# Two ratios and one weight of the filler order in the mixer stage of a two-layer hybrid encoder

## The chip, the core and the metric

The kernel runs on one core of a Trainium2 chip. TensorE (PE in the profile) does the matmuls, VectorE (DVE) and ScalarE (ACT) the elementwise work, GpSimd (POOL) a few masks and powers, SyncE (SP) issues most DMAs. The metric is the device time of one execution in microseconds; the time before is the median of three runs.

## The reference

The input is 256 tokens of width 1024 (fp32), and there are two layers. Each layer is

```
x = x + 0.5 * rms_norm(swiglu(rms_norm(x)))          # feed-forward, width 2816
z = rms_norm(x) @ w_in                                # one wide projection
y = concat(conv(z), retention(z), rwkv7(z), mlstm(z)) @ w_out
x = x + rms_norm(y)
x = x + 0.5 * rms_norm(swiglu(rms_norm(x)))          # second feed-forward
```

The four mixers have 256 channels each (4 heads of 64). All of them read columns of the same z:

```
conv:      zb * (conv1d_width3(zc * zh) + bias)                    # three projections of 256 columns
retention: rotary q, k; decay masks forward and backward; rms norm of the heads, silu gate
rwkv7:     a state S per head, forward and backward over the 256 tokens:
           S = S * w_t - (S kk_t)(kk_t a_t)^T + v_t k_t^T ;  out_t = S r_t
           then group norm, bonus and gate
mlstm:     chunks of 128; weights exp(d_log - running max) from input and forget gates,
           (q k^T * weights) v over a normalizer, forward and backward
```

## The kernel before

Everything stays on chip; the weights stream through. A 512 KB piece of a weight matrix comes by DMA on SP's queue into one of four raw buffers, ACT casts it to a rounded "hi" part and DVE forms the rest as "lo" (line 259), and every large product is done as hi x hi + hi x lo + lo x hi (three matmuls). PE's order of work is the main thing that the kernel decides. A planner places the instructions: program order is their priority, and an instruction that the planner's own estimate does not have ready lets a later one pass.

A layer is feed-forward, mixers, feed-forward. In the mixer stage the RWKV recurrence is the long chain of small dependent steps. It is solved in blocks of 64 tokens (four blocks, n = 0 to 3, two directions d): masked products of keys and queries (pgr), a triangular inverse built from 16x16 pieces (L937 pe, L949, L955, L976, L985, each a flood of 32x32 tiles), pakv (L997), and then the chain proper: pwc, pu, psn and oT (L1013 to L1053), where each step reads the state that the step before left. After it come RWKV's norm and gate (L1061 on).

The other three mixers are written as Python generators, and so is RWKV. Each `yield` hands back a weight, meant as the TensorE time in us of what was just emitted. In the first half (up to "quads", after L937) RWKV runs beside `fill1`, in the second beside `fill2`:

```
fill2 = seq_(mix(seq_((1.0 for i in range(1)), ro, mlstm()), conv(), R2), project())
```

Two ratios set the order in `fill2`. The loop over `rwkv()` adds up RWKV's weights (tm) and the weights of what was emitted beside it (tf), and once `RATIO2 * tm` is `GRAIN` (0.8) ahead of tf it emits from `fill2` until it has caught up. Inside, `mix` runs retention's end (ro) and mLSTM as its first and conv as its second part: conv is emitted until its own sum has reached `R2` times that of the first. What is left of `fill2` when RWKV has been emitted is drained behind it.

Names that the change and the prediction touch:

- conv (L1272): six projections of 128 columns, pz (L388): 8 k's of three matmuls each, a yield of 0.64 every two k's; after three of them an elementwise block (up, yc) on DVE and ACT.
- mlstm (L1161): waits (yield 0.3) until RWKV's side has formed MR, the gates' running maxima; then four broadcasts of two matmuls each, pmb (L1174 and 1175), which ACT turns into the weights wf and wfh; scores pss (L1097), products pom (L1214), and `finish`, whose transposes are ptf (L786).
- project (L1337): the first rows of w_out, ym (L1334), which read the mixers' outputs yT in the order retention, conv, mLSTM, RWKV.

PSUM has two buffers "d" (pz, later y of the first 128 tokens), two "a" (pmb, pss, pom, later y of the second), three "y" for RWKV and one "o".

Of the kernel before, what the change touches and what calls it, by code (L numbers as in the profile page):

```python
# [105 lines left out]
def tile_encoder(ctx: ExitStack, tc: tile.TileContext, x_in, wffn, win, wout, gains, params, idn, cst, rel, out, dbg=None):  # L106
# [13 lines left out]
    def tt(out, a, b, op, eng=V):  # L120
        eng.tensor_tensor(out=out, in0=a, in1=b, op=op)  # L121

    def mul(out, a, b, eng=V):
        tt(out, a, b, ALU.mult, eng)

    def add(out, a, b, eng=V):
        tt(out, a, b, ALU.add, eng)
# [10 lines left out]
    def stt(out, a, s, b, op0, op1):  # L138
        V.scalar_tensor_tensor(out=out, in0=a, scalar=s, in1=b, op0=op0, op1=op1)

    def act(out, a, f, **kw):
        return A.activation(out, a, f, **kw)  # L142
# [10 lines left out]
    def m4(shape, dt=F32, name="m4"):  # L153
        return bigp.tile(shape, dt, tag="m4", bufs=13, name=name)
# [10 lines left out]
    def a1(name, shape=(P, S), dt=F32):  # L165
        return sp.tile(list(shape), dt, tag="a1", bufs=3, name=name)

    def dump(name, ap):
        if name in dbg:
            nc.sync.dma_start(out=dbg[name], in_=ap)  # L170
# [19 lines left out]
    def c_(n):  # L190
        o, w = _COFF[n]
        return C[:, o:o + w]
# [200 lines left out]

    TA, TB, TC, SG = 4, 2, 7, 2
    NPRO, NEPI, SPLITC, WARM, W_FIN, ZW = 3, 7, 4, 6, 6.0, 2
    RATIO, RATIO2, W_PREP, W_INV, GRAIN, R1, R2, WQ, QG, KD = 0.8, 0.6, 8, 12, 0.8, 1.4, 1.2, 0.12, 8, 2

    def ffn(hold, l, j, XT, before1, before2, ahead, after, first, last, mix_next):

# [177 lines left out]
    def mixers(hold, l, XT, before2, ahead, after):  # L577
# [193 lines left out]
        def finish(o_, gate, m, scale=None, tag="a"):  # L771

            sq_ = m4([P, 2, S], name="sq_")
            act(sq_, o_, AF.Square, scale=0.125)
            ms = sp.tile([P, 8], F32, tag="ms8", bufs=2, name="ms8")
            red(ms, sq_.rearrange("p a (h v) -> p (a h) v", v=HD))
            ts(ms, ms, RMS_EPS, ALU.add)
            r = rstd(ms, 8, "r8")
            mul(gate, gate, o_)
            g4 = gate.rearrange("p a (h v) -> p (a h) v", v=HD)  # L780
            mul(g4, g4, r.rearrange("p (h o) -> p h o", o=1).broadcast_to([P, 8, HD]))
            yield W_FIN
            pt = ps.tile([P, 2, S], F32, tag=tag, bufs={"a": PA, "o": 1}[tag], name="ptf")
            for c in range(2):
                for tk in range(2):
                    T.transpose(pt[:, c, tk * P:(tk + 1) * P], gate[:, tk, c * P:(c + 1) * P], ident)  # L786
            new_yt(m)
            if scale is None:
                split_out(yT[m], pt)
            else:  # L790
                for c in range(2):
                    act(yT[m][:, 0, c, :], pt[:, c, :], AF.Copy, scale=scale[:, c:c + 1])
                    stt(yT[m][:, 1, c, :], pt[:, c, :], scale[:, c:c + 1], f(yT[m][:, 0, c, :]), ALU.mult, ALU.subtract)
# [298 lines left out]
        def scores(t, sk, name):  # L1092

            pq = [ps.tile([P, 2, S], F32, tag="a", bufs=PA, name=f"{name}{hp}") for hp in range(2)]
            for p in range(2):
                for hp in range(2):
                    T.matmul(pq[hp][:, p, :], lhsT=t[half[hp], 2 + p, sk * P:(sk + 1) * P], rhs=t[half[hp], p, :],  # L1097
                             start=p == 0, stop=True, skip_group_check=True)
            yield 0.86
            return pq  # L1100
# [60 lines left out]
        def mlstm():  # L1161
            while "MR" not in hold:
                yield 0.3
            MR = hold["MR"]

            toff = [[0, P], [0, 0]]
            tn = [[S, P], [P, S]]
            wfh = m4([P, 2, H, P], name="wfh")
            wf = [[m4([P, H, S], name="wf0"), wfh[:, 0]], [wfh[:, 1], m4([P, H, S], name="wf1")]]
            for d in range(2):  # L1170
                for hp in range(2):
                    pm_ = ps.tile([P, 2, S], F32, tag="a", bufs=PA, name="pmb")
                    for i in range(2):
                        j = 4 * d + 2 * hp + i  # L1174
                        T.matmul(pm_[:, i, :], lhsT=pair[64:128, j:j + 1].broadcast_to([64, P]), rhs=MR[64:128, d, :],
                                 start=i == 0, stop=True, skip_group_check=True)
                    yield 0.22
                    if d == 0 and hp == 0:
                        pc = ps.tile([P, 2, 16], F32, tag="o", bufs=1, name="pc")
                        for tk in range(2):  # L1180
                            T.matmul(pc[:, tk, :], lhsT=gT[:, tk * P:(tk + 1) * P], rhs=c_("sel"), start=tk == 0, stop=True,
                                     skip_group_check=True)
                        V.tensor_copy(out=cc, in_=pc[:, :, 0:8])
                        act(em, pc[:, :, 8:16], AF.Exp, scale=-1.0)
                    for i in range(2):
                        h = 2 * hp + i
                        j = 4 * d + h
                        for sk in range(2):
                            t0 = toff[d][sk]
                            act(wf[d][sk][:, h, :], pm_[:, i, t0:t0 + tn[d][sk]], AF.Exp, scale=-1.0,  # L1190
                                             bias=cc[:, sk, j:j + 1])
                for sk in range(2):
                    o0 = sk * P - toff[d][sk]
                    v_ = wf[d][sk][:, :, o0:o0 + P]
                    G.affine_select(out=v_, in_=v_, pattern=[[0, H], [1 if d == 0 else -1, P]], compare_op=ALU.is_ge,
                                    fill=0.0, base=0, channel_multiplier=-1 if d == 0 else 1)
            for sk in range(2):
                pss = yield from scores(mq, sk, "pss")
                for hp in range(2):
                    ps_ = pss[hp]  # L1200
                    for d in range(2):
                        t0 = toff[d][sk]
                        wv = wf[d][sk].rearrange("p (a b) t -> p a b t", b=2)[:, :, hp, :]
                        stt(wv, ps_[:, :, t0:t0 + tn[d][sk]], 0.125, wv, ALU.mult, ALU.mult)
            hsum = m4([P, 2, H, HD], name="hsum")
            for tk in range(2):
                for d in range(2):
                    po = ps.tile([P, H, HD + 1], F32, tag="a", bufs=PA, name="pom")
                    sks = [sk for sk in range(2) if (sk <= tk if d == 0 else sk >= tk)]
                    for h in range(H):  # L1210
                        for sk in sks:
                            o0 = tk * P - toff[d][sk]
                            for c in range(2):
                                T.matmul(po[half[c], h, :], lhsT=wf[d][sk][:, h, o0 + 64 * c:o0 + 64 * c + 64], rhs=v1[:, sk, h, :],  # L1214
                                         start=h == 0 and sk == sks[0], stop=sk == sks[-1], skip_group_check=True)
                        yield 0.17 * len(sks)
                    dn = sp.tile([P, H], F32, tag="dn", bufs=4, name="dn")
                    act(dn, po[:, :, HD], AF.Abs)
                    tt(dn, dn, em[:, tk, 4 * d:4 * d + 4], ALU.max)
                    V.reciprocal(out=dn, in_=dn)  # L1220
                    db = dn.rearrange("p (h o) -> p h o", o=1).broadcast_to([P, H, HD])
                    if d == 0:
                        mul(hsum[:, tk], po[:, :, 0:HD], db)
                    else:
                        ob = a1("ob", (P, H, HD))
                        mul(ob, po[:, :, 0:HD], db)
                        add(hsum[:, tk], hsum[:, tk], ob)

            yield from finish(hsum.rearrange("p a h v -> p a (h v)"), og, 3, PR("mn"), "o")
            if l == 0:  # L1230
                dump("y3", yT[3].bitcast(F32))
# [105 lines left out]
        def project():  # L1337
# [3 lines left out]
            for i, tk in ((0, 0), (1, 0), (2, 0), (3, 0), (0, 1), (1, 1), (4, 0), (5, 0)):  # L1341
# [5 lines left out]
                yield 0.64  # L1347

        fill2 = seq_(mix(seq_((1.0 for i in range(1)), ro, mlstm()), conv(), R2), project())
        tm = tf = 0.0  # L1350
        rest, ratio = fill1, RATIO
# [179 lines left out]
```

## Time and profile before

| what | us |
|---|---|
| median of three runs | 1164.4 |
| the runs | 1164.4, 1154.44, 1165.07 |
| profiled execution, as a whole | 1157.71 |
| its span, first to last instruction | 1156.0 |
| PE busy / DVE busy / ACT busy in the span | 1116.3 / 787.4 / 653.5 |
| mean granted TensorE clock | 0.988 |

The profile is of one execution. In a row of groups stand line, engine, operation, output<-input, tile sizes (rows*columns of the array, then the operand), the count, and behind the bar the busy time in us, the mean duration in ns, and the idle time of the engine before it with what ended it. In a table of stretches stand the stretch (from the span's start, in us), its length, then busy time and count per engine, the granted TensorE clock, the busy share of the DMA engines and GB/s. In the order of time stand start, duration, and the instruction with its count. A row of waits is: who, for whom, us in total, times, longest. Matmuls overlap: the time that one holds the array is read from start to start, and a busy PE is not PE at its peak.

### The profile page before, as it was taken

To read this page: it belongs to the slowest core of one execution; us is meant where nothing else is said; L and a number is where in the kernel's file an instruction comes from. 1 tells how busy PE (TensorE), PEld (TensorE's weight loads), DVE (VectorE), ACT (ScalarE), POOL (GpSimd) and SP (SyncE) were. 2 spreads that over 40 slices of the span, in tenths; PEclk is the share of its full clock that TensorE was granted. 3 is DMA by queue.
4 is the path that set the end of the run, shared out by engine and by line. 5 is a ranking of instruction groups with operands and counts; after the bars stand their busy time and mean duration, and the time that the engine had idled before them with its cause. 6 is when DMAs were issued, how large, how long until landed. Compare 5 with 4: busy or idle time off the path is not lost.

```text
span 1156.0 us, 20352 instructions
## 1 busy us (share of the span) xinstructions
PE 1116.3 (97%) x8083; PEld 954.3 (83%) x8083; DVE 787.4 (68%) x1371; ACT 653.5 (57%) x1193; POOL 51.4 (4%) x87
## 2 busy tenths in 40 slices
PE   8999999999899999999899999999989999999997
PEld 6888887897878788888798888879868778888886
DVE  6666566798867856566666656667895578566663
ACT  7575555777435755454555555568764157555562
POOL 0000000012000000000000000000301000000000
PEclk9999999999999999999999999999998799999999
DMA  7856554432323666655546655625242136665641
GB/s 259 278 188 202 181 189 157 145 125 90 114 72 108 202 222 193 203 174 199 179 149 207 215 186 186 209 73 185 74 159 63 56 127 205 204 196 185 197 163 37
DMA packets 53535, 189.46 MB, mean 164 GB/s; under 512 B 6200, under 2 KB 6848, under 8 KB 53440
## 3 DMA queue, kind: packets, MB, share of 16 engines
q1 hardware_dynamic: 51120, 181.28, 47.8%
q10 hardware_dynamic: 2320, 6.89, 1.8%
q8 instruction: 63, 1.03, 0.3%
q14 instruction: 32, 0.26, 0.1%
HBM read 187.10 MB, written 1.05 MB: 163 GB/s over the span
## 4 chain that ended last, share of the span: by engine, by line
PE 60%; DVE 12%; DMA 12%; ACT 8%; issue 6%; POOL 1%; SPq 0%; POOLq 0%; ACTq 0%; DVEq 0%
PE pg L472 16%; PE y L495 14%; DMA f_raw<-in_wffn_dram 11%; PE pz L388 9%; PE pg L474 8%; DVE f_lo L259 4%; ACT f_hi L142 4%; PE pgh L444 2%; DVE i_lo L259 1%; PE pss L1097 1%; PE pvg L594 1%; PE ym L1334 1%; ACT i_hi L142 1%; ACT jk L142 1%; DVE gu L121 1%
## 5 line engine op out<-in xcount | busy, mean ns | idle before, releaser
L259 DVE TENSOR_TENSOR f_lo<-f_raw,f_hi 128x1024 fp32r<-128x1024 f32 (+1 forms) x280 | 323.0, 1162 | 195.6 <-ACT f_hi L142 194.9
L472 PE MATMUL pg<-XT,f_hi 128*128 128x512 f32 x1232 | 387.4, 396 | 1.4 <-DVE gu L121 1.3
L142 ACT ACTIVATE f_hi<-f_raw 128x1024 fp32r<-128x1024 f32 (+1 forms) x280 | 279.0, 1007 | 137.8 <-DMA f_raw<-in_wffn_dram 116.6
L474 PEld LDWEIGHTS pg<-XT,f_lo 128*128 128x128 f32 x1232 | 231.3, 188 | 54.0
L474 PE MATMUL pg<-XT,f_lo 128*128 128x256 f32 x1232 | 242.2, 278 | 0.0
L495 PE MATMUL y<-f_hi,hT 128*128 128x512 f32 x704 | 232.6, 392 | 3.8 <-ACT hT L142 2.7
L472 PEld LDWEIGHTS pg<-XT,f_hi 128*128 128x128 f32 x1232 | 192.6, 189 | 7.4 <-DVE gu L121 2.2
L495 PEld LDWEIGHTS y<-f_hi,hT 128*128 128x128 f32 x704 | 131.6, 188 | 31.0 <-ACT hT L142 4.0
L388 PE MATMUL pz<-XT,i_hi 128*128 128x256 f32 x704 | 139.8, 295 | 2.2 <-DVE rvg L121 1.4
L495 PE MATMUL y<-f_lo,hT 128*128 128x512 f32 x352 | 137.3, 391 | 0.0
L388 PEld LDWEIGHTS pz<-XT,i_hi 128*128 128x128 f32 x704 | 111.4, 193 | 10.3 <-issue 4.1
L142 ACT ACTIVATE hT<-gu 128x256 fp32r<-128x256 f32 x77 | 32.1, 417 | 130.8 <-DVE gu L121 130.8
L388 PE MATMUL pz<-XT,i_lo 128*128 128x256 f32 x352 | 101.3, 288 | 0.0
L259 DVE TENSOR_TENSOR i_lo<-i_raw,i_hi 128x1024 fp32r<-128x1024 f32 (+1 forms) x68 | 73.6, 1095 | 14.5 <-ACT i_hi L142 13.5
L142 ACT ACTIVATE i_hi<-i_raw 128x1024 fp32r<-128x1024 f32 (+1 forms) x68 | 63.5, 953 | 34.4 <-PE pz L388 22.8
L121 DVE TENSOR_TENSOR gu<-pg,gu 128x256 f32<-128x256 f32 x154 | 64.4, 418 | 16.1 <-ACT gu L142 16.1
L495 PEld LDWEIGHTS y<-f_lo,hT 128*128 128x128 f32 x352 | 66.1, 188 | 11.1 <-DVE f_lo L259 0.4
L444 PE MATMUL pgh<-f_hi,XT 128*128 128x256 f32 x352 | 69.0, 290 | 2.1 <-ACT XT L142 1.1
L388 PEld LDWEIGHTS pz<-XT,i_lo 128*128 128x128 f32 x352 | 68.0, 193 | 0.8 <-issue 0.5
L142 ACT ACTIVATE gu<-pg 128x256 f32<-128x256 f32 x154 | 56.8, 369 | 18.7 <-PE pg L474 18.7
L444 PEld LDWEIGHTS pgh<-f_hi,XT 128*128 128x128 f32 x352 | 56.6, 191 | 5.3 <-ACT XT L142 1.8
L488 DVE TENSOR_TENSOR hT<-gu,hT 128x256 fp32r<-128x256 f32 x77 | 32.8, 425 | 35.1 <-ACT hT L142 34.5
(290 smaller groups left out, 1275.7 us busy)
## 6 DMA issues: line engine op xcount, KB each, us to landing
f_raw<-in_wffn_dram SPq DMA_DIRECT2D x262, 512.0 KB, 4.4
i_raw<-in_win_dram SPq DMA_DIRECT2D x60, 512.0 KB, 4.0
o_raw<-in_wout_dram SPq DMA_DIRECT2D x16, 512.0 KB, 3.7
gain<-in_gains_dram ACTq DMA_DIRECT2D x11, 512.0 KB, 4.9
x<-in_x_dram SPq DMA_DIRECT2D x4, 256.0 KB, 4.3
f_raw<-in_wffn_dram SPq DMA_DIRECT2D x4, 256.0 KB, 5.1
rl<-in_rel_dram ACTq DMA_DIRECT2D x2, 384.0 KB, 3.2
C<-in_cst_dram SPq DMA_DIRECT2D x1, 573.0 KB, 6.9
```

The lines of the kernel that those rows point to most:

```text
L121: eng.tensor_tensor(out=out, in0=a, in1=b, op=op)
L142: return A.activation(out, a, f, **kw)
L259: V.tensor_tensor(out=lo[:, cs], in0=r[:, cs], in1=f(hi[:, cs]), op=ALU.subtract)))
L388: T.matmul(dst, lhsT=w[a][:, k * P:(k + 1) * P], rhs=xt(XT, k, b), start=n == 0, stop=n == 23)
L444: T.matmul(pg, lhsT=xt(XT, k, a)[:, tk * P:(tk + 1) * P], rhs=w[b][:, c:c + 256], start=n == 0, stop=n == 23)
L472: T.matmul(pg, lhsT=w[0][:, c:c + P], rhs=xt2(XT, k + i), start=k + i == 0, stop=False, skip_group_check=True)
L474: T.matmul(pg[:, 0, :], lhsT=w[1][:, c:c + P], rhs=xt(XT, k + i, 0), start=False, stop=k + i == 7, skip_group_check=True)
L488: V.tensor_tensor(out=hT[:, 1, :], in0=h, in1=f(hT[:, 0, :]), op=ALU.subtract))
L495: ins = T.matmul(y[tk][h], lhsT=hts[fb][:, a, tk * P:(tk + 1) * P], rhs=ws[fb][2][b][:, h * 512:(h + 1) * 512], start=fb == 0 and i == 0, ...
L594: T.matmul(pv[tk], lhsT=xt(XT, k, a)[:, tk * P:(tk + 1) * P], rhs=w[b][:, (k % 2) * 512:(k % 2 + 1) * 512], start=k == 0 and i == 0, stop= ...
L1097: T.matmul(pq[hp][:, p, :], lhsT=t[half[hp], 2 + p, sk * P:(sk + 1) * P], rhs=t[half[hp], p, :], start=p == 0, stop=True, skip_group_check ...
L1334: T.matmul(y[tk][h], lhsT=yT[(1, 0, 3, 2)[i // 2]][:, a, i % 2, tk * P:(tk + 1) * P], rhs=wo[i][b][:, h * 512:(h + 1) * 512], start=i == 0 ...
```

## The change

Three numbers of the second half of the mixer stage change, in both layers:

- RATIO2 0.6 to 0.75: per unit of RWKV's weight, more of `fill2` is emitted beside it.
- R2 1.2 to 1.45: per unit of the weight of retention's end and mLSTM, more of conv is emitted.
- mLSTM's four broadcasts pmb yield 0.5 instead of 0.22 each, so more of conv goes behind each of them, and they use up more of what may be emitted beside RWKV.

No instruction is added or taken away; only the emission order, and with it the planner's order, changes.

```diff
@@ -393,7 +393,7 @@
     NPRO, NEPI, SPLITC, WARM, W_FIN, ZW = 3, 7, 4, 6, 6.0, 2
-    RATIO, RATIO2, W_PREP, W_INV, GRAIN, R1, R2, WQ, QG, KD = 0.8, 0.6, 8, 12, 0.8, 1.4, 1.2, 0.12, 8, 2
+    RATIO, RATIO2, W_PREP, W_INV, GRAIN, R1, R2, WQ, QG, KD = 0.8, 0.75, 8, 12, 0.8, 1.4, 1.45, 0.12, 8, 2
@@ -1174,7 +1174,7 @@
                         T.matmul(pm_[:, i, :], lhsT=pair[64:128, j:j + 1].broadcast_to([64, P]), rhs=MR[64:128, d, :],
                                  start=i == 0, stop=True, skip_group_check=True)
-                    yield 0.22
+                    yield 0.5
```

## The prediction

> **What bounds the kernel now.** I read the page first (busy shares, granted clock), then the busy time by stretch around the second half of each mixer stage, the PE groups inside one thin stretch, what PE waited for, and PE's order of work.
>
> ```profile
> span 1156.0 us, 20352 instructions
> PE 1116.3 (97%) x8083; PEld 954.3 (83%) x8083; DVE 787.4 (68%) x1371; ACT 653.5 (57%) x1193; POOL 51.4 (4%) x87
> PEclk9999999999999999999999999999998799999999
> ```
>
> TensorE is the bound: 97% busy over 1156.0 us; the execution as a whole took 1157.71 us, so 1.7 us lie around the span. The clock row has one dent, in the slices that hold the second half of layer 1's mixers. The diff touches only that half (layer 0: 298 to 382 us; layer 1: 864 to 949).
>
> What PE waits for between 296 and 385 us, layer 0's half with a margin:
>
> ```profile
> PE pt L314 <- DVE xg L301: 1.8, 1, 1.8
> PE ptf L786 <- DVE og L121: 1.1, 1, 1.1
> PE pe L949 <- issue: 0.7, 1, 0.7
> PE pe L955 <- issue: 0.5, 1, 0.5
> PE pe L949 <- DVE En L943: 0.4, 1, 0.4
> PE pe L937 <- ACT Dn L921: 0.3, 1, 0.3
> ```
>
> So 4.8 us per layer is all that better filling could win, and most of it is outside the change's reach: pt belongs to the next norm, L937 and L949's wait for En come before a larger share of conv work is handed out, and "issue" waits for no other engine. Only ptf's 1.1 us hangs on the order in question. In the RWKV chain itself there is nothing to fill, as busy time by stretch shows (columns: length, then busy time of each engine with its count, granted clock, DMA):
>
> ```profile
> core 0: us, PE busy (x) PEld busy (x) DVE busy (x) ACT busy (x) POOL busy (x), PEclk, DMA share, GB/s
> 314.89:322.04 7.15, 7.15 (x145) 5.98 (x144) 3.29 (x6) 4.60 (x16) 1.23 (x2) 1.00 0.26 79
> 322.04:350.00 27.96, 27.96 (x404) 22.03 (x402) 18.06 (x51) 7.65 (x22) 1.36 (x4) 1.00 0.24 74
> 320.05:335.67 15.62, 15.62 (x197) 11.57 (x195) 9.58 (x24) 5.91 (x17) 2.34 (x4) 1.00 0.09 33
> 885.13:912.43 27.30, 27.30 (x197) 19.67 (x195) 10.21 (x25) 5.98 (x17) 2.34 (x4) 0.50 0.05 18
> ```
>
> The last two rows are the same 197 matmuls in layer 0 and in layer 1. With the clock at 1.00 they take 15.62 us, at 0.50 they take 27.30. One such stretch costs 27.30 - 15.62 = 11.7 us (0.75 us per us of covered work), more than twice all the waits of a layer. The clock falls where layer 0 stands at 320.05, which is 5.2 us into the first of these rows, 314.89 to 322.04. There PE does this (busy time, mean ns, idle time before):
>
> ```profile
> L997 PE MATMUL pakv<-UV,GP 64*64 64x64 f32 x64 | 3.4, 226 | 0.0
> L1175 PE MATMUL pmb<-MR,pair 64*128 64x256 f32 x8 | 1.7, 314 | 0.0
> L985 PE MATMUL pe<-D64T,F__3413 32*32 32x32 f32 x64 | 1.4, 192 | 0.0
> L388 PE MATMUL pz<-XT,i_lo 128*128 128x256 f32 x2 | 0.8, 384 | 0.0
> L388 PE MATMUL pz<-XT,i_hi 128*128 128x256 f32 x3 | 0.7, 279 | 0.0
> L1181 PE MATMUL pc<-C,gA 128*128 128x16 f32 x4 | 0.6, 268 | 0.0
> ```
>
> All tiles there are a quarter, a half or a sixteenth of the 128x128 array, but for five pz (conv projections) and the small pc. Layer 0 has the same order and kept its clock. So the fall has a part of chance, and an array thinly used for some microseconds is its likely condition; idle time is not, for there is none.
>
> **How the profiled time stands to the runs.** Runs of 1154.44, 1164.40 and 1165.07 us form two groups 10.3 us apart, close to one 11.7 us stretch. The profile (1157.71, one stretch) lies 0.3% above the lower and 0.6% below the upper group. I read: one stretch at 1154 to 1158, two (one per layer) at 1164 to 1170, none at 1157.7 - 11.7 = 1146.0, or 1143 from the run. That makes 1, 1, 2 and 2 stretches in four executions, 6 of 8 chances.
>
> **The change, part by part.** I walked the weights of the generators by hand. RWKV's steps after "quads" weigh 4 x 3.84 + 4 x 0.8 + 2 x 0.32 + 12.48 = 31.7. A ratio of 0.6 lets 19.0 of other work run beside them, 0.75 lets 23.8. Conv has 6 projections of 8 k's, 3 matmuls each (144). With the new R2 and the heavier broadcasts too, 42 of its 48 k's are handed out before the chain ends, where it was 32; before L976 it is 22, where it was 16. L388's matmuls alone bear the old count out:
>
> ```profile
> 298.00:359.19 61.19, 24.75 (x154) 19.87 (x154) 1.00 0.25 77
> 350.00:359.19 9.19, 4.96 (x37) 4.48 (x36) 1.00 0.03 12
> ```
>
> Of the 154, ten still belong to mLSTM's projections; 154 - 10 - 37 = 107, or 36 k's, lie before 350, where the chain ends. So the planner pulls about four k's ahead of the weights when a small step isn't ready, and my order is right only to about that much.
>
> *What moves at no cost.* No matmul and no DMA is added or removed. Conv's six weight pieces are issued earlier on SP's queue, where only w_out's pieces stand behind them; the gain pieces go through ACT's queue. The cover is that ACT and DVE are far from full in the chain (7.65 and 18.06 of 27.96 us); without it PE would wait for one cast or take the next pom. Conv's first elementwise block moves ahead of the chain, the second stays behind it.
>
> *Cuts.* Evener means more and shorter runs of pz between steps of other tile shapes. PE in order of time (start, duration):
>
> ```profile
> 299.19 0.39 PE L388 MATMUL pz<-XT,i_lo 128*128 128x256 f32 x1
> ...
> 332.30 0.38 PE L388 MATMUL pz<-XT,i_lo 128*128 128x256 f32 x1
> 332.61 0.34 PE L1038 MATMUL psn<-UV,bkT 128*64 128x64 f32 x4
> ...
> 355.89 0.39 PE L1214 MATMUL pom<-v,wf 128*64 128x65 f32 x6
> 356.21 0.51 PE L388 MATMUL pz<-XT,i_hi 128*128 128x256 f32 x2
> ...
> 359.07 0.28 PE L388 MATMUL pz<-XT,i_lo 128*128 128x256 f32 x1
> 359.19 0.40 PE L1334 MATMUL ym<-o_hi,yT 128*128 128x512 f32 x1
> ...
> 363.73 0.66 PE L786 MATMUL ptf<-ident,og 128*128 128x128 f32 x4 [1.15 <-DVE og L121]
> ...
> 373.29 0.61 PE L1334 MATMUL ym<-o_hi,yT 128*128 128x512 f32 x2
> 373.75 0.39 PE L1334 MATMUL ym<-o_lo,yT 128*128 128x512 f32 x1
> 373.97 0.61 PE L1334 MATMUL ym<-o_hi,yT 128*128 128x512 f32 x2
> ```
>
> In the long run from 356.21 to 359.19 a pz starts every 0.12 us (24 in 2.98); the lone one at 332.30 holds the array for 0.31. A run of pz therefore costs about 0.19 us beyond its matmuls. By hand there are 13 such runs before and 17 after; the trace has 25 (the first at 299.19, the last at 356.21), so by the same ratio it would be 33. That gives between nothing, if the planner merges them again, and 8 x 0.19 = 1.5 us per layer. I take 4 x 0.19 = 0.75, the hand count, or 1.5 for both layers (0 to 3.0).
>
> *The wait for ptf.* The last pom ends at 356.28 and ptf starts at 363.73: mLSTM's finish takes 7.45 us. Today 2.98 us of pz, 3.4 us of ym and 1.15 us of nothing lie beside it. After the change conv's last k's come before the last pom, so that cover is gone. In its place conv's output is ready early: 24 ym for retention and 24 for conv, at 0.68 / 3 = 0.227 us each, make 10.9 us, more than 7.45. If conv's elementwise tail is late, only the first 24 (5.4 us) are there, and 2.0 us stay open. That is -1.15 to +0.9 per layer. I take -0.6, half the wait, since the planner puts ptf where its own estimate has it ready; -1.2 for both (-2.3 to +1.8).
>
> *The chain's end.* Behind the chain 10 k's fewer (3.6 us) are left. The last w_out rows need RWKV's norm, which lasts from the copy of oT to its yT; PE still has 10.9 us of ym and 11 of 16 pom steps before it needs them. I take 0.
>
> *The clock.* In the old order come L976, half of L985, three broadcasts, two k's, the rest of L985, all pakv, the first pu, two k's: the 7.1 us of the groups above almost in one piece. In the new one come L976, two broadcasts, two k's, L985, half of pakv, two k's, a broadcast, the other half, chain steps, the last broadcast, two k's. The longest thin piece is then at most L985 1.4 + half of pakv 1.7 + four pmb 0.85 + pc 0.6 = 4.6 us. If the chance goes with the length, 0.75 per layer becomes 0.75 x 4.6 / 7.1 = 0.48: none in 27% of the executions, one in 50%, two in 23%. The ends are none ever (-11.7 us against the profile) and two ever (+11.7).
>
> **Sum.** Cuts +1.5, ptf -1.2, the rest 0: +0.3 us. With one stretch that is 1157.7 + 0.3 = 1158.0 by the profile and 1154.4 + 0.3 = 1154.7 by the run of its group. Forecast: one stretch, **1156 us**; with the bounds of cuts and ptf (-2.3 to +4.8) its own range is 1152 to 1161. Against the median of 1164.4 that is 0.7% less.
>
> **Rivals.**
> *None.* The six pz cut the thin piece for good, and the clock stays up in both layers: 1156 - 11.7 = 1144. For it: layer 0 kept its clock with the longer piece. Against: 4.6 us of quarter and sixteenth tiles are still there. Chance 0.26.
>
> *As often as before.* The planner fills by readiness, pulls the same k's to the same places and leaves the thin piece as it is, or the clock doesn't depend on it: two stretches, 1156 + 11.7 = 1168, less some for the spread of the runs (1164 to 1169). For it: the four k's pulled ahead. Against: the fall came inside the thin piece and nowhere else. Chance 0.20.
> The Trainium skill ("TensorE: Matmul & The Clock Gate", section "Why this matters for your kernels") has the clock fall after idle gaps of some 3 us; by that rule this change, which leaves no such gap before or after, would leave the clock and the time as they are. The trace disagrees on the condition: PE's idle time is 0.0 in all six groups of the thin piece, and the clock fell all the same.
>
> *Slower: the clock doesn't come back.* It came back at 912.43, behind the first longer run of pz in the chain. With pz dealt out in sixes, the array may stay too thin in the whole chain, and the half clock last until the long run after it: 356.21 - 320.05 = 36.2 us of work at 0.75 each, 27 us instead of 11.7. In both layers: 1144 + 54 = 1198. Over 1% slower (1176) it is from (1176 - 1144) / 0.75 = 43 us of covered work, 21 a layer against 15.6 today. For it: 1.00 of clock came only after 27 us, though PE was busy throughout. Against: the chain as a whole gets 30 pz more, and by hand two runs of twelve are in it. Chance 0.10.
>
> **How the numbers follow.** Forecast 0.44, none 0.26, as before 0.20, not coming back 0.10. The range 1143 to 1168 holds the forecast, all but 0.04 of "none" and of "as before" each, and leaves out the slow rival: 0.82. One per cent, about what a measurement of this kernel can tell from no change, is 1152.8 and 1176.0. Faster: "none" 0.26 and the low edge of the forecast 0.10, 0.36. Slower: 0.10. Within: 0.34 + 0.20 = 0.54.
>
> **What would show it.** Right: in the granted clock at most one half-clock stretch where the old kernel had one or two; in the PE groups of any 4 us between L976 and the first pu more pz than now; about 126 of conv's matmuls before the chain's end; ptf's wait under 1.1 us; more but shorter runs of pz, and the span without half clock within 3 us of 1144.3 (1156.0 - 11.7). Wrong: two stretches in most executions, a stretch much longer than 27 us, a new wait of PE for og, xc or a pz copy above 2 us, or a new thin piece late in the chain.

## The result, and the profile after

The changed kernel takes 1165.51 us (median of 20 executions, 1158.13 to 1172.39), the kernel before 1155.09 us beside it (20 executions): 1.009 of the time, 95% interval 1.0067 to 1.0112. (The three runs known ahead, with a median of 1164.4, are three of these 20, and two of them are among the five slowest.) The forecast was 1156 us, 0.7% less than those 1164.4; measured is 0.9% more than before. The profiled execution of the changed kernel took 1159.15 us. Every ratio here and below leaves out the slow executions (over 1.5% above the fastest of their kernel) and is not the quotient of the two medians, so the two can differ.

Busy time and granted clock on its page:

```profile
span 1157.4 us, 20348 instructions
PE 1113.1 (96%) x8083; PEld 951.9 (82%) x8083; DVE 788.9 (68%) x1371; ACT 652.2 (56%) x1193; POOL 52.2 (5%) x87
PEclk9999999999999899999999999999999998999999
```

TensorE is busy 3.2 us less than before, yet the span is 1.4 us longer. The dent that the clock row had in layer 1's recurrence is gone, and two shallow ones stand in the slices around 387 and 963 us. So the span alone hides two things that nearly cancel in this one execution. The busy time by stretch separates them: first the kernel before, from the first L937 to the first matmul of the next feed-forward (L444) in layer 0 and 1, then the same two stretches of the changed kernel and two stretches in which its clock is halved.

```profile
297.97:385.91 87.94, 83.32 (x1274) 69.19 (x1275) 63.98 (x132) 42.35 (x92) 8.01 (x13) 1.00 0.33 105
864.02:962.19 98.17, 94.58 (x1275) 77.06 (x1275) 64.08 (x132) 42.56 (x92) 7.63 (x8) 0.86 0.29 94
```

```profile
298.75:390.06 91.31, 84.62 (x1274) 69.32 (x1274) 64.19 (x133) 42.46 (x94) 8.99 (x14) 0.98 0.32 104
870.98:962.10 91.12, 84.42 (x1274) 69.10 (x1274) 64.28 (x133) 42.55 (x94) 8.66 (x9) 0.99 0.33 104
386.80:393.60 6.80, 5.40 (x22) 4.71 (x23) 5.92 (x11) 4.50 (x9) 1.53 (x2) 0.50 0.63 176
960.30:967.10 6.80, 6.50 (x29) 5.80 (x28) 6.38 (x12) 3.74 (x8) 0.86 (x1) 0.50 0.79 255
```

The second row of before holds the long half-clock stretch, worth 11.7 us; without it the stage is 98.17 - 11.7 = 86.5 us. Call the length of such a row the stage. It went from 87.94 to 91.31 in layer 0 and from 86.5 to 91.12 in layer 1: 3.4 + 4.6 = 8.0 us more. The five pieces of the span add up: 0.8 (up to the first L937), 3.4, 2.8 (between the stages), -7.0 (layer 1 with its half clock) and 1.5 (the rest) make 1.4 us.

What PE waits for: the longest two rows of the changed kernel's stage in layer 0, then in layer 1, and the longest row of the kernel before in layer 1:

```profile
PE pt L314 <- DVE xg L301: 4.3, 1, 4.3
PE ptf L786 <- DVE og L121: 1.2, 1, 1.2
...
PE pt L314 <- DVE xg L301: 4.1, 1, 4.1
PE ptf L786 <- DVE og L121: 1.1, 1, 1.1
...
PE pt L314 <- DVE xg L301: 1.3, 1, 1.3
```

The wait for ptf, on which the prediction spent a term, is what it was (1.15 us before). The wait that grew is the one for xg, the normalized first 128 tokens: 1.8 to 4.3 us in layer 0, 1.3 to 4.1 in layer 1. PE in order of time, pt in the kernel before and then both waits in the changed kernel:

```profile
383.14 1.09 PE L314 MATMUL pt<-ident,xg 128*128 128x128 f32 x8 [1.75 <-DVE xg L301]
...
369.95 0.66 PE L786 MATMUL ptf<-ident,og 128*128 128x128 f32 x4 [1.15 <-DVE og L121]
...
383.38 0.39 PE L1334 MATMUL ym<-o_hi,yT 128*128 128x512 f32 x1
388.04 1.97 PE L314 MATMUL pt<-ident,xg 128*128 128x128 f32 x8 [4.27 <-DVE xg L301]
```

Every product of w_out is done at 383.77 and PE stands idle for 4.27 us. The eight transposes pt then take 1.97 us, in the kernel before 1.09: the clock fell at 386.80, while PE stood idle. Of the 8.0 us that the two stages grew by, 2.5 + 2.8 are these longer waits and 0.9 + 0.9 the slower pt; the 0.9 left lie in smaller differences and in the estimate of 11.7.

Why ptf is late shows on DVE. Kernel before, in order of time, from the last products of mLSTM to the last multiply of its finish:

```profile
357.76 0.42 DVE L121 TENSOR_TENSOR ob<-pom,dn 128x256 f32<-128x256 f32 x1
358.22 0.43 DVE L121 TENSOR_TENSOR hsum<-hsum,ob 128x256 f32<-128x256 f32 x1
...
360.36 0.42 DVE L121 TENSOR_TENSOR up<-pz,cc 128x256 f32<-128x256 f32 x1
...
362.98 0.69 DVE L121 TENSOR_TENSOR og<-og,r 128x512 f32<-128x512 f32 x1 [1.54 <-POOL r L121]
```

The changed kernel:

```profile
356.12 0.42 DVE L121 TENSOR_TENSOR up<-pz,cc 128x256 f32<-128x256 f32 x1
...
360.91 0.42 DVE L121 TENSOR_TENSOR yT<-yc,yT 128x256 fp32r<-128x256 f32 x1
361.25 0.69 DVE L121 TENSOR_TENSOR xc<-xc,bg 128x512 f32<-128x512 f32 x1
361.85 0.42 DVE L121 TENSOR_TENSOR hsum<-pom,dn 128x256 f32<-128x256 f32 x1
...
363.57 0.68 DVE L259 TENSOR_TENSOR o_lo<-o_raw,o_hi 128x512 fp32r<-128x512 f32 x1
364.17 0.42 DVE L121 TENSOR_TENSOR hsum<-hsum,ob 128x256 f32<-128x256 f32 x1
...
369.20 0.69 DVE L121 TENSOR_TENSOR og<-og,r 128x512 f32<-128x512 f32 x1 [1.54 <-POOL r L121]
```

Before, conv's second block (up, yc) follows mLSTM's sum hsum; now it stands ahead of it. From the end of the last pom to the start of that last hsum it was 358.22 - 356.28 = 1.9 us and is 364.17 - 358.34 = 5.8 us.

What that does to PE can be counted in the program's own order of PE. Call y0 the 48 products of w_out (ym) for the first 128 tokens, y1 the 48 for the second. Before, 14 ym come before ptf (13 of y0, 1 of y1), and 36 of y1 are left behind the last of y0. After the change 39 come before ptf (24 and 15), and 17 of y1 are left. At 0.227 us each that is 8.2 us of work behind y[0] before and 3.9 us after. The norm of y[0] has to fit into that. It starts on ACT with the first read of ym, before and after:

```profile
376.08 0.58 ACT L142 ACTIVATE jk<-ym 128x512 bf16<-128x512 f32 x1
...
380.91 0.58 ACT L142 ACTIVATE jk<-ym 128x512 bf16<-128x512 f32 x1
```

From there to pt it takes 383.14 - 376.08 = 7.1 us before and 388.04 - 380.91 = 7.1 us after. The norm is as long as it was, and its cover is gone.

### The profile page after: what moved, and what is told of

Its sections match the earlier page's. It is cut to its first block, busy times and chain, and to the rows that moved or that the text cites. A ratio compares the mean times of both kernels' runs of the same rounds, so it can differ in the third digit from the quotient of the medians.

```text
span 1157.4 us, 20348 instructions
## 1 busy us (share of the span) xinstructions
PE 1113.1 (96%) x8083; PEld 951.9 (82%) x8083; DVE 788.9 (68%) x1371; ACT 652.2 (56%) x1193; POOL 52.2 (5%) x87
## 5 line engine op out<-in xcount | busy, mean ns | idle before, releaser
L388 PE MATMUL pz<-XT,i_hi 128*128 128x256 f32 x704 | 138.4, 292 | 2.4 <-DVE rvg L121 1.6
L388 PEld LDWEIGHTS pz<-XT,i_hi 128*128 128x128 f32 x704 | 109.7, 190 | 9.0 <-issue 2.5
L388 PE MATMUL pz<-XT,i_lo 128*128 128x256 f32 x352 | 99.8, 283 | 0.0
L444 PE MATMUL pgh<-f_hi,XT 128*128 128x256 f32 x352 | 71.9, 298 | 3.2 <-ACT XT L142 1.9
L388 PEld LDWEIGHTS pz<-XT,i_lo 128*128 128x128 f32 x352 | 67.1, 191 | 0.3
L444 PEld LDWEIGHTS pgh<-f_hi,XT 128*128 128x128 f32 x352 | 59.1, 200 | 7.0 <-ACT XT L142 3.4
```

The lines of the kernel that those rows point to most:

```text
L388: T.matmul(dst, lhsT=w[a][:, k * P:(k + 1) * P], rhs=xt(XT, k, b), start=n == 0, stop=n == 23)
L444: T.matmul(pg, lhsT=xt(XT, k, a)[:, tk * P:(tk + 1) * P], rhs=w[b][:, c:c + 256], start=n == 0, stop=n == 23)
```

## The experiments

Theory A is that mLSTM's finish comes too late and PE then waits for the norm of y[0]. Theory B puts the loss on the clock, theory C on more and shorter runs of pz.

Half-clock time below is (1 - mean granted clock) x 2 x span of an execution. The stages are in us, layer 0 / layer 1; a star marks one that holds a long half-clock stretch. "y1 left" is the count just explained.

| kernel | RATIO2, R2, weight | ratio to before (95%) | y1 left | wait pt | stages |
|---|---|---|---|---|---|
| before | 0.6, 1.2, 0.22 | 1 | 36 | 1.8 / 1.3 | 87.9 / 98.2* |
| e1 | 0.6, 1.45, 0.22 | 0.9982 (0.9945 to 1.0018) | 32 | 0.9 / 0.6 | 102.6* / 87.0 |
| e2 | 0.75, 1.2, 0.22 | 0.9950 (0.9916 to 0.9985) | 30 | 0.6 / 0.6 | 86.0 / 85.1 |
| e3 | 0.6, 1.2, 0.5 | 0.9901 (0.9867 to 0.9935) | 35 | 1.4 / 1.5 | 87.2 / 85.2 |
| e5, first pair | 0.75, 1.45, 0.22 | 0.9990 (0.9947 to 1.0033) | 26 | 0.8 / 1.0 | 99.1* / 87.9 |
| e5, second pair | 0.75, 1.2, 0.5 | 1.0024 (0.9989 to 1.0058) | 16 | 4.0 / 4.3 | 90.4 / 89.4 |
| e5, third pair | 0.6, 1.45, 0.5 | 0.9946 (0.9911 to 0.9982) | 23 | 1.2 / 1.6 | 85.0 / 85.6 |
| after | 0.75, 1.45, 0.5 | 1.0090 (1.0067 to 1.0112) | 17 | 4.3 / 4.1 | 91.3 / 91.1 |

**One edit at a time.**

```diff
-    ... 0.8, 0.6, 8, 12, 0.8, 1.4, 1.2, 0.12, 8, 2
+    ... 0.8, 0.6, 8, 12, 0.8, 1.4, 1.45, 0.12, 8, 2    # e1: R2 alone
+    ... 0.8, 0.75, 8, 12, 0.8, 1.4, 1.2, 0.12, 8, 2    # e2: RATIO2 alone
-                    yield 0.22
+                    yield 0.5                          # e3: the broadcasts' weight alone
```

> The kernel before with R2 1.45 alone. Theory A (the change makes mLSTM's finish late: the transposes ptf and with them the last rows of the first 128 tokens' output, and the norm behind them waits): by the instruction order 27 of the 96 ym stand ahead of ptf here, 14 in the kernel before and 39 in the changed one. 13 x 0.227 = 3.0 us later per layer, about half of the changed kernel's 4 us: +2 us per layer, +3 to +5 us in all, 0.3% to 0.4% slower than before, and a wait of pt for xg of 2.5 to 3.5 us. Theory B (the clock: the wait itself costs little, the lost time is half-clock time): no more than 1 us outside half-clock stretches, time follows the granted clock. Theory C (more cuts between pz and other tiles): up to +1.5 us per layer whatever ptf does.

> The kernel before with RATIO2 0.75 alone. Theory A: all pom stand ahead of the chain's end here and only 7 of 96 ym ahead of ptf (14 before), so mLSTM's finish comes earlier: ptf's and pt's waits at or under those of the kernel before, 0 to -2 us per layer, 0 to 0.3% faster than before. Theory B: the number of pz between L976 and the first pu is 28 (25 before), the clock falls there as often as before, same time. Theory C: +0.5 to +1.5 us per layer, as conv is cut into shorter runs here too.

> The kernel before with the broadcasts' weight 0.5 alone. Theory A: 21 of 96 ym ahead of ptf (14 before): 1.6 us later per layer, +0.5 to +1.5 us per layer, 0.1% to 0.3% slower than before. Theory B: only 12 pz stand between L976 and the first pu (25 before), so if the clock falls where the array is thin, it falls here more often: a long half-clock stretch in at least half of the runs, 0.5% or more slower. Theory C: 0 to +1 us per layer.

Medians of 1152.3, 1149.14 and 1144.37 us against 1153.45 of the kernel before. No single edit shows a loss, and two of the three gain. Theory A missed here: with 27 of the 96 ym ahead of ptf, e1 was to wait 2.5 to 3.5 us (0.9 and 0.6 came) and lose 0.3% to 0.4%, and e3, with 21, was to lose 0.1% to 0.3%; only e2 came out as it said. Theory B missed too, with a loss of 0.5% or more for e3. Both stages of e3:

```profile
302.30:389.54 87.24, 82.67 (x1274) 69.34 (x1275) 63.90 (x133) 42.63 (x91) 8.00 (x13) 0.98 0.34 107
867.28:952.51 85.23, 81.31 (x1274) 67.93 (x1275) 63.82 (x133) 42.67 (x91) 7.62 (x8) 1.00 0.36 110
```

So the loss is one of the three together. If the three effects simply added up, the sum would be 0.983. Why e3 alone is 9 us faster is not shown: its stages are 0.7 and 1.3 us shorter than those of the kernel before.

**Two edits at a time** (the values stand in the table; the edits are the lines above).

> RATIO2 0.75 and R2 1.45, broadcasts still 0.22. The order of work here: conv's last projections come before mLSTM's last products (no pz behind the last pom, 24 in the kernel before), 34 of the 96 products of w_out are used up before ptf (14 before, 39 with all three edits). Theory A (mLSTM's finish becomes the last thing on the path, and too little of w_out is left to cover the norm behind y[0]): most of the loss is here, 1156 to 1159 us, and PE waits over 3 us for the norm in each layer. Theory B (the loss comes from the clock's falls and hangs on the broadcasts' weight): near RATIO2 alone, 1148 to 1152, wait under 2 us.

> RATIO2 0.75 and the broadcasts' weight 0.5, R2 still 1.2. The order of work: 6 pz are left behind the last pom and conv's second block stands on DVE partly ahead of mLSTM's finish; 42 of 96 products of w_out lie before ptf. Theory A: a wait of 3 us or more for the norm, 1152 to 1157 us, slower than either edit alone (1149.1 and 1144.4). If the two gains simply added up it would be 1140 us.

> R2 1.45 and the broadcasts' weight 0.5, RATIO2 still 0.6. The order of work: no pz behind the last pom, 34 of 96 products of w_out before ptf, but 34 pz are still behind the recurrence's last step. Theory A: a wait of 2 to 4 us for the norm, 1148 to 1155 us. If the two effects simply added up it would be 1143 us.

Medians of 1154.42, 1160.63 and 1151.21 us against 1157.08 beside them. Two of theory A's three expectations missed: RATIO2 with R2 (over 3 us of wait expected) keeps short waits (0.8 and 1.0 us), and so does R2 with the weight (2 to 4 us expected, 1.2 and 1.6 measured), though in both 34 ym stand ahead of ptf and no pz is left behind the last pom. Those two counts were the wrong ones. The count that separates the cases is y1 left; it was found from these runs. The second pair alone shows the wait (and its time lies above the 1152 to 1157 us expected). PE at layer 0's pt in it:

```profile
388.21 1.97 PE L314 MATMUL pt<-ident,xg 128*128 128x128 f32 x8 [3.97 <-DVE xg L301]
```

Where 16 or 17 of y1 are left the wait is 4.0 to 4.3 us; where 23 or more are left it is 1.8 at most. Above that the two don't go together closely: with 35 and 36 left the planner puts 9 and 8 of them behind pt, and the wait is 1.3 to 1.8 us. From ACT's first read of y[0] to pt the norm takes 7.0 to 7.6 us in both layers of every kernel in the table and of those below, and y1 must cover it.

**Only mLSTM's finish made later.** The kernel before, with eight multiplications by 1.0 on DVE:

```diff
+            hf = hsum.rearrange("p a h v -> p (a h v)")
+            for _ in range(8):
+                ts(hf, hf, 1.0, ALU.mult)
             yield from finish(hsum.rearrange("p a h v -> p a (h v)"), og, 3, PR("mn"), "o")
```

> The kernel before, with nothing changed but eight multiplications of hsum by 1.0 on DVE ahead of mLSTM's finish, about 0.5 us each, so mLSTM's output comes some 4 us later (in the changed kernel it comes 3.8 us later after its last product: 6.2 against 2.4 us). PE's other order stays, 24 pz still lie behind the last pom; the products of w_out before ptf go from 14 to 41. Theory A: PE's wait for the norm goes from 1.8 and 1.3 to 3 us or more in each layer, the clock falls behind that wait, and the time rises by 4 to 9 us, to 1157 to 1162. Theory C (more and shorter runs of pz cost the time): no change, 1153.

1162.32 us against 1157.08: 1.0095 (1.0046 to 1.0145; by the medians 1.0045). The delay as the trace has it, and layer 0's and layer 1's wait and stage:

```profile
L134 DVE TENSOR_SCALAR hsum<-hsum 128x512 f32<-128x512 f32 x8 | 3.4, 421 | 0.0
```

```profile
PE pt L314 <- DVE xg L301: 4.1, 1, 4.1
...
PE pt L314 <- DVE xg L301: 3.9, 1, 3.9
```

```profile
302.40:394.37 91.97, 84.71 (x1274) 69.66 (x1274) 66.21 (x141) 42.76 (x94) 9.05 (x14) 0.98 0.32 103
874.96:977.62 102.66, 95.97 (x1275) 77.51 (x1275) 66.19 (x141) 42.90 (x94) 8.48 (x9) 0.85 0.28 92
```

None of the three numbers is changed here, conv still comes last, and 3.4 us of extra work ahead of mLSTM's finish are enough to make the changed kernel's picture: 41 ym ahead of ptf, 16 of y1 left, a wait of 4 us, and a stage of 92.0 us (in layer 1, 102.66 - 11.7 = 91.0 without its long half-clock stretch). That is theory A, with its size: 4.0 to 4.5 us per layer. Theory C expected no change here.

**Conv's second block held back.** The changed kernel, with that block tied on DVE behind the last multiply of mLSTM's finish:

An excerpt (the block itself becomes a function that conv puts into the list `late`):

```diff
-            yield from finish(hsum..., og, 3, PR("mn"), "o")
+            g = finish(hsum..., og, 3, PR("mn"), "o")
+            yield next(g)
+            while not late:
+                yield 0.3
+            with held(fin[0]):        # fin: finish's last multiply
+                late.pop()()          # late: conv's second elementwise block
+            yield from g
```

> The changed kernel with one thing undone: conv's second elementwise block is held on DVE behind the last multiply of mLSTM's finish, where the kernel before has it. PE's order of pz in the chain stays the changed one. Theory A: DVE reaches the finish 2.5 us sooner, 27 instead of 39 ym stand ahead of ptf; the wait of pt for xg falls from 4.2 to 2 to 3 us and the time by 1.5 to 2.5 us per layer: 0.3% to 0.5% faster than the changed kernel, still 0.4% to 0.6% slower than before. Theory B and C: the same time as the changed kernel, 0.9% slower than before, within 1 us per layer.

1158.64 us against 1153.45: 1.0049 (1.0017 to 1.0082), about half the loss. But the waits show that it went another way than theory A has it (the product of w_out is L1351 here, ptf L788):

```profile
PE ym L1351 <- ACT yT L142: 1.6, 1, 1.6
PE ptf L788 <- DVE og L783: 1.2, 1, 1.2
...
PE pt L314 <- DVE xg L301: 0.5, 1, 0.5
PE ym L1351 <- DVE yT L121: 0.5, 1, 0.5
...
PE ym L1351 <- DVE o_lo L259: 0.4, 1, 0.4
```

The wait for the norm is down to 0.5 us (28 of y1 are left), and 1.6 + 0.5 = 2.1 us of waiting for conv's own output and 0.4 for a piece of w_out have come in its place. The stages stay long, 91.2 us (with 3.4 us at half clock in it) and 90.0. With both blocks needed, putting one behind the other mostly moves the wait. Where the gain comes from is not shown. No wait is long here, no fall of the clock stands behind one, and the median half-clock time of an execution is 8.1 us, against 29.1 in the changed kernel; but none of the ten executions has over 20.9 us of it, so the long stretch in the recurrence is missing too, perhaps by chance.

**The price of the clock behind the wait.** The changed kernel, with ten matmuls that nobody reads behind the last ym:

```diff
+        dummy = ps.tile([P, 512], F32, tag="o", bufs=1, name="dummy")
+        for n in range(10):
+            T.matmul(dummy, lhsT=yT[1][:, 0, 0, 0:P], rhs=wo[1][0][:, 0:512], start=True, stop=True)
         return y, None
```

> The changed kernel, with ten more matmuls of 128x512 per layer that nobody reads, into a free PSUM buffer, placed between the last product of w_out and the norm's transposes pt. They fill 10 x 0.227 = 2.3 us of PE's wait of 4.3 us and leave 2 us. Nothing comes earlier by itself. If the half-clock stretch of 6.8 us behind that wait comes from PE standing idle, it disappears in both layers, and the time falls by 2 x 6.8 x 0.33 to 0.5 = 4.5 to 6.8 us against the changed kernel, to about 1155 to 1161 (1.001 to 1.005 of the kernel before). If the stretch has another cause, the time stays at 1.009 of the kernel before.

1164.21 us against 1153.23: 1.0082 (1.0042 to 1.0123), a miss. In the profiled execution the stretches did vanish:

```profile
385.02 2.43 PE L1390 MATMUL dummy<-o_hi,yT 128*128 128x512 f32 x10
388.93 1.09 PE L314 MATMUL pt<-ident,xg 128*128 128x128 f32 x8 [1.48 <-DVE xg L301]
390.95 0.38 PE L444 MATMUL pgh<-f_hi,XT 128*128 128x256 f32 x1 [0.93 <-ACT XT L142]
```

pt runs at full speed, but L444 now waits 0.93 us for the copies of pt, which the slow transposes had hidden, and the stages are 91.4 and 91.0 us as before. Behind the stages the changed kernel loses 480.92 - 479.21 = 1.7 us to this one up to layer 1's first L937, and 0.8 us from layer 1's L444 to the end. I had priced a microsecond at half clock at 0.33 to 0.5 us wherever it falls; here it is worth 0.8 to at most 1.7 us per 6.8. (The first also holds two short falls of 3.4 us that the other lacks.) In this profile the waiting costs, and the clock behind it adds little. By the times alone up to 5 us of gain aren't excluded (the interval reaches down to 1.0042).

**RATIO2 with a smaller weight.** The bad pair with 0.35 in place of 0.5, and a version with RATIO2 0.70:

```diff
-    ... 0.8, 0.6, 8, 12, 0.8, 1.4, 1.2, 0.12, 8, 2
+    ... 0.8, 0.75, 8, 12, 0.8, 1.4, 1.2, 0.12, 8, 2    # the other: 0.7
-                    yield 0.22
+                    yield 0.35
```

> RATIO2 0.75 and R2 1.2 as in the bad pair, but the broadcasts' weight 0.35 in place of 0.5. In the order of work 29 products of the second 128 tokens are left behind y[0]'s last one (16 in the pair with 0.5, 36 before), 12 pz lie behind the last pom. Theory A: the wait for the norm falls from 4.0 and 4.3 us to 0.5 to 1.5, no fall of the clock behind it, and the time is under that of the kernel before, 0.988 to 0.996 of it. If RATIO2 with a heavier weight costs time for another reason (more and shorter runs of pz, thin tiles), it stays at or above 1.000.

> RATIO2 0.70, R2 1.2, the broadcasts' weight 0.35: a version between those that were faster. 29 products left behind y[0]'s last one, 12 pz behind the last pom, 24 behind the recurrence's last step. Theory A: the wait for the norm 0.5 to 1.5 us, 0.986 to 0.994 of the kernel before.

1149.59 us, 0.9958 (0.9923 to 0.9993), and 1153.36 us, 0.9982 (0.9949 to 1.0014), against 1153.23. The first is what theory A expected: 29 of y1 left, waits of 0.8 and 1.1 us, stages of 86.4 and 85.7 us; the same RATIO2 is good or bad by what it leaves. The second has the short waits (0.8 and 0.5) and stages (86.9 and 85.9) but missed its ratio by 0.4%.

**Where the clock falls in longer executions.** In 21 of the 87 executions of the kernel before that ran beside these experiments, the half-clock time was 32 us or more. The changed kernel's profile showed no long stretch, but its executions had up to 46.8 us. Four more profiled executions, three of the changed kernel (f1, f2, f3) and one of the kernel with the ten matmuls (f4):

> The changed kernel once more, one look, to see where its clock falls in an execution with much half clock. Its twenty executions have 13.9 to 46.8 us of half clock (worked out as (1 - mean granted clock) x 2 x span), of which 13.6 are the two stretches behind the waits for the norm. Theory B (the long half-clock stretch in the recurrence's thin piece is still there, as in the kernel before): in an execution of 1165 us or more a stretch of some 27 us starts 20 to 22 us behind the first L937 of a layer. Theory D (it is gone, and the rest is many short stretches): stretches of 3.4 and 6.8 us only.

> As the look before: a stretch of some 27 us 20 to 22 us behind L937 by theory B, stretches of 3.4 and 6.8 us only by theory D.

> As the look before: a stretch of some 27 us 20 to 22 us behind L937 by theory B, stretches of 3.4 and 6.8 us only by theory D.

> The kernel with ten unread matmuls ahead of the norm's transposes once more, one look. Four of its ten executions have 32.6 us of half clock or more though its waits for the norm are short. Theory B: in such an execution (1164 us or more) one stretch of some 27 us 20 to 22 us behind L937. Theory D: short stretches only.

Times of 1168.02, 1165.32, 1168.03 and 1171.32 us. Neither theory holds as put: in three of the four (f1, f2, f4) a stretch starts 21.1 to 21.7 us behind layer 1's first L937, where theory B has it, but it lasts 13.7 us, not 27.3. Layer 1's stage and the stretch in f2:

```profile
872.70:969.18 96.48, 90.22 (x1274) 74.09 (x1274) 64.30 (x133) 42.87 (x94) 8.68 (x9) 0.91 0.31 98
894.00:907.70 13.70, 13.70 (x148) 11.77 (x148) 5.51 (x11) 8.09 (x25) 2.64 (x4) 0.50 0.13 39
```

It costs 96.48 - 91.12 = 5.4 us. PE in it, in order of time, first and last row of two runs of pz:

```profile
899.21 0.79 PE L388 MATMUL pz<-XT,i_hi 128*128 128x256 f32 x2
...
900.44 0.41 PE L388 MATMUL pz<-XT,i_lo 128*128 128x256 f32 x1
...
904.09 0.58 PE L388 MATMUL pz<-XT,i_hi 128*128 128x256 f32 x1
...
907.02 0.41 PE L388 MATMUL pz<-XT,i_lo 128*128 128x256 f32 x1
```

Six pz at 899 didn't bring the clock back; a run of 14, from 904.09 to 907.02, stands just ahead of its return at 907.7. The kernel before, layer 1, again first and last row of two runs:

```profile
888.53 0.79 PE L388 MATMUL pz<-XT,i_hi 128*128 128x256 f32 x2
...
890.62 0.41 PE L388 MATMUL pz<-XT,i_hi 128*128 128x256 f32 x1
...
910.11 0.58 PE L388 MATMUL pz<-XT,i_hi 128*128 128x256 f32 x1
...
911.35 0.41 PE L388 MATMUL pz<-XT,i_hi 128*128 128x256 f32 x1
```

Here ten pz at 888.53 didn't bring it back, and six stand ahead of its return at 912.4; in e1 the last ones ahead of its return, at 355.2, are three. So the length of such a run doesn't settle it. Why the stretch is half as long in the changed kernel stays open.

How often the stretch comes does not go with the number of pz in the thin piece either. Between L976 and the first pu stand 12 in e3 and in the third pair, and none of their twenty executions has more than 23 us of half clock; of the kernel before, with 25, it is 21 of 87 that have 32 us or more, of e2, with 28, none of ten, and of the first pair, with 30, 3 of ten. The prediction and theory B had it the other way round, and what makes the clock fall there stays open too.

All three of these executions of the changed kernel have the wait for the norm in both layers, and behind each of the six a half-clock stretch of 6.8 or 10.2 us. With the changed kernel's own profile, the second pair and the delayed finish that is 12 of 12 waits of 3.7 us or more, while 3 of 22 stages with a wait under 2 us have one. This is the rule of the Trainium skill ("TensorE: Matmul & The Clock Gate", section "Why this matters for your kernels"), that the clock falls after idle gaps of some 3 us: for these waits the traces agree with it. The stretch in the thin piece is not covered by it: PE is busy 13.70 of 13.70 us there.

## Why the prediction was wrong, point by point

**"The wait for ptf" is the step that failed.** It priced PE's own wait for ptf, took 24 + 24 products of w_out as the cover for mLSTM's finish, and came to -0.6 us per layer. The cover was used as foreseen (39 products stand ahead of ptf, whose wait stayed at 1.15 us). But half of those 48 belong to the second 128 tokens, and they were the cover of the next wait, that for the norm of y[0]. They were counted as free. And the wait for that norm had been set aside at the start ("pt belongs to the next norm", outside the change's reach), so no term of the sum stood for it. The term should have followed the chain one step on: mLSTM's sum 3.9 us later after the last pom, y[0] 4.0 us later from the first L937 (ACT reads it at 380.91 - 298.75 = 82.2 us, before at 376.08 - 297.97 = 78.1), 17 in place of 36 products left, and a wait for xg of 4.3 us. Measured: 3.4 and 4.6 us more per layer, where the text had -0.6. It also gave +0.9 as its worst end, with a late elementwise tail of conv; it did not see that this tail would stand on DVE ahead of mLSTM's finish and make the finish itself late.

**"The chain's end: I take 0"** looked only at RWKV's norm and gate, which indeed make no new wait. **"What moves at no cost"** left out DVE's order, which is where the block that moved got in the way.

**No rival had it.** "None" and "as often as before" were both about how often the long stretch comes, and the profiles show that it still comes and is shorter. The list of what would show the prediction wrong did: "a new wait of PE for og, xc or a pz copy above 2 us" is the right kind of wait in the wrong place. The slower rival put its price on the clock and had it the wrong way round: full clock came back sooner.

**The hand count of the order.** 126 conv matmuls were to lie before the chain's end; in the program's order 138 of 144 lie before the last step of the recurrence, since the planner pulls more ahead than the weights say. Between L976 and the first pu there are 19 pz, fewer than the 25 before, where more were expected. L388 in the changed kernel, up to the first ym from the first L937 and from the chain's end:

```profile
298.75:358.28 59.53, 24.98 (x154) 19.94 (x154) 1.00 0.25 80
354.27:358.28 4.01, 1.03 (x6) 0.73 (x5) 1.00 0.01 2
```

Six matmuls are left behind the chain; 37 were before (39 if one counts from the recurrence's last step itself).

**"Cuts".** The number of runs of pz in layer 0's stage is 25 in both kernels, where 29 to 33 were forecast. PE's busy time in that stage rose by 84.62 - 83.32 = 1.3 us, of which 0.9 are pt at half clock. The 0.4 left lie within the term's 0 to 1.5; the choice of 0.75 was too high.

**"The clock".** That one stretch costs 11.7 us and begins in the thin piece held: it begins there in six of the kernels run, 20.3 to 21.7 us behind the first L937. How often was read wrong: from three run times and one profile the text made 0.75 per layer, and about one execution in four has 32 us of half clock or more. Of the twenty executions of the kernel before 13 lie between 1150 and 1156 us, so the low group, read as "one stretch", is the usual one, and the forecast of 1156 us is its upper end. What the change does was wrong in kind: where the stretch comes it is half as long, 13.7 us for 5.4 us instead of 27.3 for 11.7; whether it comes more or less often these few profiles can't tell. The change was also taken to leave no long idle gap; it makes one of 4.3 and one of 4.1 us, and the clock fell in or right behind each. Without a long stretch the span was to be within 3 us of 1144.3; it is 1157.4, and 8.0 of the 13.1 us between them lie in the stages.

**The sum.** 1.5 - 1.2 + 0 = +0.3 us was forecast outside the clock; the stages show +8.0. The measured difference is 1165.51 - 1155.09 = 10.4 us. The other 2.4 us are as much as the half clock behind the stages can be (0.8 + 1.7 = 2.5 us); how the frequency and the changed length of the thin-piece stretch enter on average can't be told from four profiles. That 1165.51 lies inside the range of 1143 to 1168 is luck: the range was made of half-clock stretches that come or don't, and what happened is a longer stage.

## What to carry to other kernels

A piece of independent work can cover one wait only: before taking it as cover for an operation that becomes late, look which later wait it covers now, and follow the delay to that wait. When filler is dealt out differently, check the order on the elementwise engine as well as on TensorE: a filler's own elementwise tail, brought forward, queues ahead of the critical one. Tuning numbers that each help (0.995 and 0.990 here) can together cross a threshold; of the versions run here, the broadcasts' weight of 0.5 alone is the best, 0.990 (0.987 to 0.994) of the kernel before.

## What the runs showed of the hardware that was not expected

Apart from one that the end of the kernel cuts off, half-clock stretches come in multiples of about 3.41 us: 3.4, 6.8, 10.2, 13.7, 27.3 and 34.1 us were seen. Their cost depends on where they fall: 27.3 us in the recurrence cost 11.7, 6.8 us at the start of the feed-forward 0.8 to 1.7, where PE partly waits for copies anyway.

A busy PE does not always bring the clock back. In the thin piece it stayed at half for 13.7 us (changed kernel), 27.3 us (before) and 34.1 us (R2 alone) with PE never idle; how many 128x128 matmuls stood ahead of its return differed (14, six and three). And a wait under 2 us did not always go without a fall: in f4, the kernel with ten unread matmuls, the clock fell for 3.4 and 6.8 us behind waits of 1.7 and 1.6 us, though nothing shows that these waits were the cause.
